# Last projections of a two-layer decoder trunk: a norm's offset kept in PSUM, no GpSimd, and a final product done row by row

## The chip, the cores and the metric

One core of one Trainium2 chip runs the whole kernel in one launch. The time is device microseconds of one execution; for each kernel the median of several runs is given. The profile is of one execution of its own.

## The reference

The input is 1024 tokens of width 1024 in float32. Two layers follow each other; every sub-layer is `x <- LayerNorm(alpha * x + sublayer(x))`, with alpha = 4^0.25. Layer 0 is a sparse attention, layer 1 a gated linear recurrence, and each is followed by a SwiGLU feed-forward of width 2816:

```python
def layer_norm(x, g, b):
    mu = mean(x); var = mean(square(x - mu))
    return (x - mu) * rsqrt(var + 1e-5) * g + b
h = layer_norm(ALPHA * h + mixer(h), ln_g[l, 0], ln_b[l, 0])
h = layer_norm(ALPHA * h + (silu(h @ w_gate) * (h @ w_up)) @ w_down, ln_g[l, 1], ln_b[l, 1])
```

The change concerns the last projection of a sub-layer (`@ w_down`, and `@ w_o` of the recurrence), the residual sum and norm behind it, and the way in which the normalised rows become operands of the next layer's first product.

## The kernel before

All large matrix products after the attention are float32 products made of three matmuls each (`mm3`, lines 103 to 105): both operands are split into a rounded high part (ScalarE, L447) and a rest (VectorE, L448) by `split2`. On top of this, a product is done by a Strassen scheme with 2 x 2 blocks: seven products, numbered 1 to 7, of sums and differences of blocks. `ORDER` and `X` name the operands.

The function `last` does a last projection. It is called three times: for layer 0's feed-forward (11 slices of the inner dimension for each of the seven products), for the recurrence's output projection (4 slices), and for layer 1's feed-forward (11 slices, whose result is the kernel's output). The 1024 tokens are eight rows of 128, `rows[0]` to `rows[7]`; rows 0 to 3 are here called early, rows 4 to 7 late, since the products are taken in the order 1, 2, 6, 5, 3, 7, 4 and the early rows are complete after product 3, the late rows after product 4. Each product runs over slices q, and in a slice over four blocks of rows m, with three matmuls of 128 x 512 each; so a slice is 12 matmuls. For each slice `load` fetches two 128 x 512 blocks, `prepare` splits them two slices ahead, `product` multiplies. The sums go from PSUM into `rows` by VectorE (`scaled`, L714, and `add`, L715); the rows themselves, the residual, are fetched from DRAM (L694), where `keep` (L832) put them.

The norm of the early rows is the generator `leave`, one for each pair of rows. It is advanced by `tick` between slices of products 7 and 4: statistics on VectorE (L790), a reciprocal root of eleven small VectorE steps (`rsqrt`, L113 to L118), one ScalarE pass (L797), then on GpSimd the multiplication by the norm's scale (L800) and the addition of its offset (L801). The row is stored (`keep`, or in the third call into the output, L805), and `features` transposes it on TensorE (L302) and forms Strassen's sums and differences on VectorE (L307), ScalarE and VectorE splitting them for the next product. The late rows go through `norm_late` (L818 to L827), which leaves the offset out of the rows. They are transposed and summed at once by `operand`: transposes of several rows add up in PSUM (L358), and the offset enters by one small product with 12 rows, `off` times `blocks` (L361), built by `parts` (L380 to L395). Because the late rows are kept without offset, the next call of `last` adds it to them on GpSimd (L704), from a broadcast load of it (L700).

In the third call, product 4's last two slices are done row by row: after the matmuls of a row comes its sum, its statistics and its part of `norm_late`.

One queue, SP's, issues all DMAs in order: loads of slices (L655, L656), of rows, of the norm's scale and offset (L709), and the stores. The pool that `last` opens takes memory that the stage before it gives back. The order in which instructions stand on each engine is set by a planner that draws on program order and on its own estimate of durations; it may move work of other parts between the steps of one.

## Time and profile before

| | before |
|---|---|
| median of 3 runs | 2712.49 us (2706.94 to 2715.37) |
| profiled execution | 2713.93 us, its span 2711.7 us |
| TensorE (PE) busy | 2530.6 us, 93% of the span |
| VectorE (DVE) busy | 2002.5 us, 74% |
| ScalarE (ACT) busy | 1130.5 us, 42% |
| GpSimd (POOL) busy | 356.1 us, 13% |
| mean granted TensorE clock | 0.960 |
| first, second, third call of `last`, about | 1115 to 1412, 1866 to 2050, 2441 to 2712 us |

In a line of the profile, the engine is followed by the source line, the operation, the tile that it writes and those that it reads, the shapes and the count. A bracket tells how long the engine was idle before the instruction and what ended that. `x` and `rows` are rows of 128 x 1024; `Y` and `M` are PSUM tiles; `w`, `ph` and `pl` are split operands; `raw` are loaded slices. Names like `DVE rows L715` on the right of an arrow are the instruction whose end was seen last before the waiting engine went on. The matmuls' ends are modelled, so busy shares of PE are read from their starts where it matters.

### The profile page before, as it was taken

Reading aid. Unit: us, or ns where it says so; the run is one execution under the profiler, and the core shown is the slowest. Engines: PE = TensorE matmul, PEld = TensorE weight load, DVE = VectorE, ACT = ScalarE, POOL = GpSimd, SP = SyncE. Lnnn points to the kernel's source line nnn. Section 1 sums busy time; section 2 is a strip of 40 time slices with the busy share of each in tenths; the row PEclk is TensorE's granted clock in tenths of the full one; section 3 lists DMA queues with packets and bytes.
Section 4 is the critical chain, followed back from the end, with each engine's and each line's share of the span. In section 5 each row is a group of like instructions: output and inputs, shape, how many; then the busy total and the mean of one; then the engine's idle time right before and its main releaser. Section 6 shows DMA issues by size and latency. Waiting matters only on the chain.

```text
span 2711.7 us, 36971 instructions
## 1 busy us (share of the span) xinstructions
PE 2530.6 (93%) x13048; PEld 2112.4 (78%) x13048; DVE 2002.5 (74%) x4007; ACT 1130.5 (42%) x2192; POOL 356.1 (13%) x382
## 2 busy tenths in 40 slices
PE   8977899999899999999899999998869999999995
PEld 7765678888888888878788888887658878888774
DVE  6599889643687876656878888887687876664766
ACT  5576667554433233343453333332344323333441
POOL 1333422110000000000302111111130000000011
PEclk9987799999899999999999999999879999999998
DMA  3213210000166753385521111113525763337653
GB/s 130 83 55 126 89 40 25 29 33 10 59 222 240 237 171 117 99 276 197 175 99 71 51 40 67 40 51 109 191 92 181 244 207 116 95 107 252 203 179 132
DMA packets 159665, 334.63 MB, mean 123 GB/s; under 512 B 16593, under 2 KB 47993, under 8 KB 151801
## 3 DMA queue, kind: packets, MB, share of 16 engines
q1 hardware_dynamic: 159480, 332.28, 36.5%
q8 instruction: 103, 1.69, 0.3%
q14 instruction: 82, 0.66, 0.1%
HBM read 233.11 MB, written 99.09 MB: 123 GB/s over the span
## 4 chain that ended last, share of the span: by engine, by line
PE 53%; DVE 16%; DMA 10%; issue 5%; POOL 2%; ACT 2%; SPq 1%; POOLq 0%; DVEq 0%; ACTq 0%
PE M L104 7%; PE M L105 7%; PE M L103 7%; PE Y L104 5%; PE Y L105 5%; PE Y L103 5%; DMA wdt<-in_wd_dram 4%; PE O L1537 4%; DMA t4q<-wdt 3%; DVE w L448 3%; PE Y L961 2%; PE L L1522 2%; DVE wdt L557 2%; PE T L1532 2%; PE Y L358 1%
## 5 line engine op out<-in xcount | busy, mean ns | idle before, releaser
L447 ACT CAST w<-raw 128x512 fp32r<-128x512 f32 (+1 forms) x377 | 292.6, 778 | 501.5 <-PE M L105 250.4
L448 DVE TENSOR_TENSOR w<-raw,w 128x512 fp32r<-128x512 f32 (+1 forms) x377 | 350.5, 932 | 180.5 <-ACT w L447 178.4
L103 PE MATMUL M<-x,w 128*128 128x512 f32 (+1 forms) x1120 | 434.0, 388 | 4.1 <-DVE e L481 2.2
L104 PE MATMUL M<-x,w 128*128 128x512 f32 (+1 forms) x1120 | 430.6, 385 | 0.0
L105 PE MATMUL M<-x,w 128*128 128x512 f32 (+1 forms) x1120 | 427.1, 382 | 2.4 <-DVE w L448 2.4
L103 PE MATMUL Y<-x,w 128*128 128x512 f32 (+1 forms) x644 | 247.5, 385 | 3.9 <-DVE e L481 2.5
L104 PE MATMUL Y<-x,w 128*128 128x512 f32 (+1 forms) x644 | 247.1, 384 | 1.8 <-DVE x L307 1.8
L105 PE MATMUL Y<-x,w 128*128 128x512 f32 (+1 forms) x644 | 246.8, 383 | 0.0
L103 PEld LDWEIGHTS M<-x,w 128*128 128x128 f32 x1120 | 212.0, 189 | 43.9 <-DVE e L481 3.5
L105 PEld LDWEIGHTS M<-x,w 128*128 128x128 f32 x1120 | 212.0, 189 | 41.4 <-DVE w L448 2.8
L104 PEld LDWEIGHTS M<-x,w 128*128 128x128 f32 x1120 | 212.3, 190 | 36.4
L447 ACT CAST w<-s 128x512 fp32r<-128x512 f32 x180 | 111.7, 621 | 307.9 <-PE M L105 87.8
L1537 PEld LDWEIGHTS O<-vv,pT 128*128 128x128 f32 x1152 | 149.2, 200 | 27.3 <-ACT pT L1534 24.1
L1537 PE MATMUL O<-vv,pT 128*128 128x64 f32 x1152 | 155.8, 283 | 5.1 <-ACT pT L1534 4.0
L448 DVE TENSOR_TENSOR w<-s,w 128x512 fp32r<-128x512 f32 x180 | 124.4, 691 | 43.6 <-ACT w L447 43.0
L103 PEld LDWEIGHTS Y<-x,w 128*128 128x128 f32 x644 | 123.0, 191 | 28.4 <-DVE e L481 3.3
L104 PEld LDWEIGHTS Y<-x,w 128*128 128x128 f32 x644 | 123.4, 192 | 25.1 <-DVE x L307 2.0
L105 PEld LDWEIGHTS Y<-x,w 128*128 128x128 f32 x644 | 123.2, 191 | 22.8
L800 POOL TENSOR_TENSOR x<-x,gb 128x1024 f32<-128x1024 f32 x12 | 32.8, 2735 | 792.4 <-ACT x L797 792.4
L1522 PE MATMUL L<-ks,qt 128*128 128x512 f32 (+5 forms) x384 | 116.4, 392 | 19.6 <-DVE nm L1524 18.4
L1534 ACT COPY pT<-T 128x512 f32<-128x512 f32 (+3 forms) x192 | 85.2, 478 | 86.5 <-PE T L1532 85.6
L1526 ACT ACTIVATE p<-p,nm 128x128 f32<-128x128 f32 (+7 forms) x128 | 99.3, 777 | 51.1 <-DVE nm L1524 50.6
(424 smaller groups left out, 5586.3 us busy)
## 6 DMA issues: line engine op xcount, KB each, us to landing
raw<-in_wgu_dram SPq DMA_DIRECT2D x44, 1024.0 KB, 6.8
wdt<-in_wd_dram SPq DMA_DIRECT2D x44, 512.0 KB, 3.9
raw<-in_wd_dram SPq DMA_DIRECT2D x66, 256.0 KB, 3.5
raw<-in_hw_dram SPq DMA_DIRECT2D x16, 1024.0 KB, 4.8
qr<-qd SPq DMA_DIRECT2D x64, 128.0 KB, 2.8
t5q<-wdt SPq DMA_DIRECT2D x26, 256.0 KB, 7.8
t7q<-wdt SPq DMA_DIRECT2D x26, 256.0 KB, 4.6
h7q<-s SPq DMA_DIRECT2D x26, 256.0 KB, 5.8
```

What stands on the lines that cost most here:

```text
L103: mm(out, a[0], b[0], start=first, stop=False, **kw)
L104: mm(out, a[0], b[1], start=False, stop=False, **kw)
L105: mm(out, a[1], b[0], start=False, stop=last, **kw)
L447: self.nc.scalar.copy(hi, x)
L448: (eng or self.nc.vector).tensor_tensor(lo, x, hi.bitcast(F32), op=ALU.subtract)
L557: sub = lambda o, a, b: v.tensor_tensor(o, a, b, op=ALU.subtract)
L961: nc.tensor.matmul(pl[rows, n, cols], lhs, rhs, start=True, stop=True)
L1522: nc.tensor.matmul(ps, s.qt[:, h % 4, :], s.ks[gi][i][:, kr], start=i == 0, stop=i == 1)
L1526: nc.scalar.activation(p, p, AF.Exp, bias=nm, scale=-1.0, accum_out=sm[:, h : h + 1])
L1532: nc.tensor.transpose(pt[:, i * P : (i + 1) * P], p[:, c : c + P], self.ident)
L1534: nc.scalar.copy(pT[:, : m * P], pt[:, : m * P])
L1537: nc.tensor.matmul(po[:, h * 64 : (h + 1) * 64], pT[:, i * P : (i + 1) * P], s.vv[:, k, gi * 64 : (gi + 1) * 64], start=k == 0, stop=k == j,)
```

## The change

In all three calls GpSimd has no more part in it. `features` and `operand` share a helper, `turn`, that transposes terms into one PSUM tile and adds the offset there; so early rows too are kept without it. `leave` is one generator for all four early rows, with one reciprocal root for all; their statistics are taken earlier, as halves of rows become complete (`count`). `norm_row` multiplies by the scale on VectorE (one operation with the mean's subtraction) and by the reciprocal root on ScalarE.

Where the norm before left an offset (the second and the third call), it is no longer added to rows: a second set of `parts`, `plus`, times alpha, enters the PSUM sums of products 2, 5 and 7 by `offset`, four products of 12 rows by 128 columns for each of the four blocks, 48 in a call.

In the second call (`nq < 8`) the early pairs' operands are made by `operand_sum` and `operand_out`, as the late pairs' are, no longer by `features`; the first seven slices are split into the standing weight slots and no longer into the pool's own tiles, and `tick` is called four times a slice instead of three.

In the third call eight of the eleven slices of product 4 are loaded and split during products 2 to 7 (`hold`), into free slots of the operands' memory; then product 4 runs row by row over all eleven slices, each row followed by its own norm, and rows are stored in halves (`norm_out`).

```diff
--- before
+++ after
@@ -286,20 +284,17 @@
-    def features(self, pool, p, rows, defer=False):
-        nc, v = self.nc, self.nc.vector
...
-                y = self.ps_y()
-                ys.append(y)
-                for k in range(4):
-                    o = (4 * i + k) * P
-                    nc.tensor.transpose(y[:, k * P : (k + 1) * P], r[:, o : o + P], self.ident)
+                ys.append(self.ps_y())
+                self.turn(ys[-1], [r[:, i * 512 : (i + 1) * 512]], off[:, i, :])
         while self.owed:
             self.owed.pop(0)()
...
@@ -334,12 +329,25 @@
+    def turn(self, y, terms, off=None):
+        mm = self.nc.tensor.matmul
+        for k in range(4):
+            c = slice(k * P, (k + 1) * P)
+            for i, x in enumerate(terms):
+                flags = dict(is_transpose=True, start=k + i == 0, stop=True, skip_group_check=True)
+                mm(y[:, c], x[:, c], self.ident, **flags)
+        if off is not None:
+            mm(y, off, self.blocks, start=False, stop=True, skip_group_check=True)
     def operand(self, p, n, rows, less, off=None):
-        nc, mm = self.nc, self.nc.tensor.matmul
+        self.operand_out(p, n, self.operand_sum(n, rows, less, off))
+    def operand_sum(self, n, rows, less, off):
         (a1, a2), (b1, b2), (l1, l2) = ((x[:, :512], x[:, 512:]) for x in (*rows, less[1]))
         terms = {
             1: (a1,),
...
@@ -351,14 +359,10 @@
-        for k in range(4):
-            c = slice(k * P, (k + 1) * P)
-            for i, x in enumerate(terms):
...
-            mm(y, off[:, i, :], self.blocks, start=False, stop=True, skip_group_check=True)
+        self.turn(y, terms, None if off is None or n in (4, 5) else off[:, {1: 0, 7: 2}.get(n, 1), :])
+        return y
...
@@ -381,11 +382,20 @@
+    def parts(self, pool, b, tag, scale=None):
...
         nc.sync.dma_start(both[:, 0:2, :], b.rearrange("(i k c) -> k i c", i=2, k=4))
+        if scale is not None:
+            v.tensor_scalar(both[:, 0:2, :], both[:, 0:2, :], scale, None, op0=ALU.mult)
         v.tensor_tensor(both[:, 2, :], both[:, 1, :], both[:, 0, :], op=ALU.subtract)
...
@@ -636,24 +646,31 @@
-        items = [(n, q) for n in (1, 2, 6, 5, 3, 7, 4) for q in range(nq)]
...
+        held = nq - 3 if out else 0
+        items = [(n, q) for n in (1, 2, 6, 5, 3, 7, 4) for q in range(held if n == 4 else 0, nq)]
...
@@ -661,13 +678,28 @@
                 ns = ((2, 3), (), (6, 7), (1, 5))[(len(items) - 1 - i) % 4]
+                if i < 7 and nq < 8:
+                    ns = ((6, 7), (2, 3), (1, 5))[i % 3]
...
+            def hold():
+                for q in range(min(held, 6)):
+                    fetch(spare[q], 4, q)
+                    yield
+                for q in range(held):
+                    x = xs[q // 4][:, q % 4]
+                    self.split2([x[:, 0], x[:, 1]], spare[q % 6])
+                    ready[4, q] = x[:, 0], x[:, 1]
+                    if q + 6 < held:
+                        fetch(spare[q], 4, q + 6)
+                    yield
...
@@ -680,31 +712,41 @@
+                    if n != 1 and q % 3 == 2:
+                        while more and next(more[0], self) is self:
+                            more.pop(0)
...
+            def offset(dst, i):
+                if self.plus is not None:
+                    for k in range(4):
+                        c = slice(k * P, (k + 1) * P)
+                        nc.tensor.matmul(
+                            dst[:, c], self.blocks[:, c], plus[:, i, :], start=False, stop=True, skip_group_check=True
+                        )
...
-            u = self.xslot(0, (P, 4, 512))
+            u = self.xslot(0, (P, 16, 512))
+            spare = [u[:, 4 + 2 * i : 6 + 2 * i] for i in range(6)]
+            if held:
+                xs = [self.xslot(g, (P, 4, 2, 2, 512), F32R) for g in (1, 2)]
+                more.append(hold())
...
+            self.picks(pool)
             if self.plus is not None:
-                w = self.tile(pool, [P, D], F32, "t")
-                nc.sync.dma_start(w, self.plus.partition_broadcast(P))
-                for p in (2, 3):
-                    for i in range(2):
-                        r = rows[p + 4 * i]
-                        gp.tensor_tensor(r, r, w, op=ALU.add)
-            self.plus = gb[1]
+                plus = self.parts(pool, self.plus, "plus", ALPHA)
+            off = self.parts(pool, gb[1], "off") if nxt else None
             wide = []
-            for i, x in enumerate(gb):
+            for i, x in enumerate(gb if out else gb[:1]):
...
@@ -713,7 +755,11 @@
+            stats = self.tile(pool, [P, 8, 2, 6], F32, "lnst")
+            stats = [stats[:, m] for m in range(8)]
+            count = lambda m, i: v.bn_stats(stats[m][:, i, :], rows[m][:, (lo, hi)[i]])
             for m in half:
+                offset(a[m], 0)
                 scaled(rows[m][:, lo], a[m])
...
@@ -727,46 +773,67 @@
+                for m in half:
+                    count(m, 0)
+                    yield
...
-            tick(8)
+            tick(12)
             for m in half:
+                offset(a[m], 1)
                 add(rows[4 + m][:, hi], a[m])
...
             for m in half:
                 add(rows[m][:, hi], a[m])
-            jobs.extend(self.leave(pool, p, [rows[m] for m in self.PAIRS[p]], wide, out) for p in range(2))
+                count(m, 1)
+            jobs.append(self.leave(pool, rows[:4], stats, wide, off, out, nq < 8))
             b = [self.ps_m() for _ in half]
-            pace = (1, 2) if nq > 8 else (3, 3)
+            pace = (1, 2) if nq > 8 else (4, 4)
             products(7, b, ticks=pace)
...
             for m in half:
                 add(rows[4 + m][:, hi], b[m])
-                stats[4 + m] = self.tile(self.small, [P, 2, 6], F32, f"lnst{m}", bufs=1)
-                v.bn_stats(stats[4 + m][:, 1, :], rows[4 + m][:, hi])
+                count(4 + m, 1)
+                offset(b[m], 0)
+            if out:
+                self.plus = None
+                prepare(len(items) - 1)
+                while jobs or more:
+                    tick()
+                    while more and next(more[0], self) is self:
+                        more.pop(0)
+                for m in half:
+                    for q in range(nq):
+                        product(4, q, m, b[m], False)
+                    add(rows[4 + m][:, lo], b[m])
+                    count(4 + m, 0)
+                    p = next(p for p in (2, 3) if 4 + m in self.PAIRS[p])
+                    rs, mv = self.norm_scale([stats[4 + m]])
+                    self.norm_out(rows[4 + m], mv[:, 0, 0:1], rs[:, 0:1], wide, out(4 + m))
+                return
+            self.plus = gb[1]
             few = 2
             products(4, b, True, nq - few, ticks=pace)
...
             for p, rs in zip((2, 3), pairs):
-                self.norm_late(p, rs, [stats[m] for m in self.PAIRS[p]], wide, out)
-                if nxt:
-                    slots = [self.tile(pool, [P, n], F32, x) for n, x in ((512, ("t4", "pl")[p - 2]), (D, ("st", "t")[p - 2]))]
-                    less.append(self.negatives(rs, slots))
+                scale, mv = self.norm_scale([stats[m] for m in self.PAIRS[p]])
+                for i in range(2):
+                    self.norm_row(p + 4 * i, rs[i], mv[:, i, 0:1], scale[:, i : i + 1], wide)
+                less.append(self.negatives(rs, self.less_slots(pool, p)))
...
@@ -774,57 +841,65 @@
+    def less_slots(self, pool, p):
+        return [self.tile(pool, [P, n], F32, x) for n, x in ((512, ("t4", "t5")[p % 2]), (D, ("st", "t")[p % 2]))]
+    def norm_scale(self, stats):
+        n = len(stats)
+        mv = self.tile(self.small, [P, 4, 2], F32, "lnmv")[:, :n]
+        for i, x in enumerate(stats):
+            self.nc.vector.bn_aggr(mv[:, i, :], x.rearrange("p a b -> p (a b)"))
+        return self.rsqrt(mv[:, :, 1], n, 1.0, LN_EPS, "ln"), mv
+    def norm_row(self, i, r, mean, scale, wide):
+        self.nc.vector.scalar_tensor_tensor(r, r, mean, wide[0], op0=ALU.subtract, op1=ALU.mult)
+        self.nc.scalar.activation(r, r, AF.Copy, scale=scale)
+        self.keep(i, r)
+    def norm_out(self, r, mean, scale, wide, dst):
+        v = self.nc.vector
+        v.scalar_tensor_tensor(r, r, mean, wide[0], op0=ALU.subtract, op1=ALU.mult)
+        for c in (slice(0, 512), slice(512, 1024)):
+            v.scalar_tensor_tensor(r[:, c], r[:, c], scale, wide[1][:, c], op0=ALU.mult, op1=ALU.add)
+            self.nc.sync.dma_start(dst[:, c], r[:, c])
+    def leave(self, pool, rows, stats, wide, off, out, summed):
+        scale, mv = self.norm_scale(stats[:4])
...
-        for i, r in enumerate(rows):
-            gp.tensor_tensor(r, r, wide[0], op=ALU.mult)
-            gp.tensor_tensor(r, r, wide[1], op=ALU.add)
-            if out is None:
-                self.keep(p + 4 * i, r)
-            else:
-                nc.sync.dma_start(out(self.PAIRS[p][i]), r)
-            yield
-        if out is None:
-            yield
-            yield
-            yield
-            yield from self.features(pool, p, rows, p == 0)
...
+        pairs = [[rows[m] for m in self.PAIRS[p]] for p in range(2)]
+        less = []
+        for p, rs in enumerate(pairs):
+            for i, m in enumerate(self.PAIRS[p]):
+                if out is not None:
+                    self.norm_out(rs[i], mv[:, m, 0:1], scale[:, m : m + 1], wide, out(m))
+                else:
+                    self.norm_row(p + 4 * i, rs[i], mv[:, m, 0:1], scale[:, m : m + 1], wide)
+                yield
+            if out is None and not summed:
+                yield
+                yield
+                yield from self.features(pool, p, rs, off)
+            elif out is None:
+                less.append(self.negatives(rs, self.less_slots(pool, p)))
+                yield
+                for n in self.ORDER[:-1]:
+                    if p == 0 and n in (1, 5, 7):
+                        self.x_out(0, n)
+                    self.operand(p, n, rs, less[p], off)
+                    yield
+        if less:
+            ys = [self.operand_sum(4, rs, l, off) for rs, l in zip(pairs, less)]
+            self.x_out(0, 4)
+            for p, y in enumerate(ys):
+                self.operand_out(p, 4, y)
...
```

More of the change, by code (lines that the diff above doesn't have):

```diff
@@ L287, in x_in, with features @@
         return x[:, part, i, k, cols]
-    def features(self, pool, p, rows, defer=False):
-        nc, v = self.nc, self.nc.vector
+    def features(self, pool, p, rows, off):
+        nc, v, defer = self.nc, self.nc.vector, p == 0
         ys = []
@@ L353, in operand, with operand_out @@
         y = self.ps_y()
[L354 to L361 removed]
+        self.turn(y, terms, None if off is None or n in (4, 5) else off[:, {1: 0, 7: 2}.get(n, 1), :])
+        return y
+    def operand_out(self, p, n, y):
         x, i = self.X[n]
@@ L370, in negatives, with picks @@
         return slots
-    def parts(self, pool, b):
+    def picks(self, pool):
         nc, v = self.nc, self.nc.vector
@@ L642, in last, with fetch @@
         half = range(4)
-        items = [(n, q) for n in (1, 2, 6, 5, 3, 7, 4) for q in range(nq)]
-        ready, raws, loaded = {}, {}, 0
-        jobs = []
+        held = nq - 3 if out else 0
+        items = [(n, q) for n in (1, 2, 6, 5, 3, 7, 4) for q in range(held if n == 4 else 0, nq)]
+        ready, raws = {}, {}
+        jobs, more = [], []
         with self.tc.tile_pool(name=self.name("la"), bufs=1, reuse_waits="tile") as pool:
-            def load(i):
-                n, q = items[i]
-                if i == 0 or (len(items) - i) % 2 == 0:
-                    self.two = self.tile(self.wp, [P, 2, 2, 512], F32, "raw", bufs=2)
-                raw = raws[i] = self.two[:, (len(items) - i) % 2]
+            def fetch(raw, n, q):
                 w = {1: (0, lo), 2: (1, lo), 3: (1, hi)}.get(n)
@@ L656, in load @@
                 nc.sync.dma_start(raw[:, 1, :], wd[2 * q + w[0]][:, w[1]] if w else wt[q][n])
+            def load(i):
+                if i == 0 or (len(items) - i) % 2 == 0:
+                    self.two = self.tile(self.wp, [P, 2, 2, 512], F32, "raw", bufs=2)
+                raws[i] = self.two[:, (len(items) - i) % 2]
+                fetch(raws[i], *items[i])
             def prepare(i):
@@ L753, in last @@
                 tick()
[L754 removed]
+            first = self.begin(nxt)
             weave(islice(first, 4))
@@ L776, in last @@
             step(half, 9)
-            if nxt:
-                for n in self.ORDER:
-                    for p in (2, 3):
-                        self.operand(p, n, pairs[p - 2], less[p - 2], off)
-    def leave(self, pool, p, rows, wide, out):
-        nc, v, gp = self.nc, self.nc.vector, self.nc.gpsimd
-        n = len(rows)
-        mv = self.tile(self.small, [P, n, 2], F32, "lnmv")
-        for i, r in enumerate(rows):
-            st = self.tile(self.small, [P, 2, 6], F32, "lnst")
-            for c in range(2):
-                v.bn_stats(st[:, c, :], r[:, c * 512 : (c + 1) * 512])
-            v.bn_aggr(mv[:, i, :], st.rearrange("p a b -> p (a b)"))
-            yield
-        rs = self.rsqrt(mv[:, :, 1], n, 1.0, LN_EPS, "ln")
-        mr = self.tile(self.small, [P, n], F32, "lnmr")
-        v.scalar_tensor_tensor(mr, mv[:, :, 0], -1.0, rs, op0=ALU.mult, op1=ALU.mult)
-        for i, r in enumerate(rows):
-            nc.scalar.activation(r, r, AF.Identity, bias=mr[:, i : i + 1], scale=rs[:, i : i + 1])
-        yield
-        for i, r in enumerate(rows):
-            gp.tensor_tensor(r, r, wide[0], op=ALU.mult)
-            gp.tensor_tensor(r, r, wide[1], op=ALU.add)
-            if out is None:
-                self.keep(p + 4 * i, r)
-            else:
-                nc.sync.dma_start(out(self.PAIRS[p][i]), r)
-            yield
-        if out is None:
-            yield
-            yield
-            yield
-            yield from self.features(pool, p, rows, p == 0)
@@ L813, in norm_late @@
-    def norm_late(self, p, rows, stats, wide, out):
-        nc, v = self.nc, self.nc.vector
-        mv = self.tile(self.small, [P, 2, 2], F32, "lnmv")
-        for i in range(2):
-            v.bn_aggr(mv[:, i, :], stats[i].rearrange("p a b -> p (a b)"))
-        rs = self.rsqrt(mv[:, :, 1], 2, 1.0, LN_EPS, "ln")
-        for i, r in enumerate(rows):
-            v.scalar_tensor_tensor(r, r, mv[:, i, 0:1], wide[0], op0=ALU.subtract, op1=ALU.mult)
-            if out is None:
-                nc.scalar.activation(r, r, AF.Copy, scale=rs[:, i : i + 1])
-                self.keep(p + 4 * i, r)
-            else:
-                v.scalar_tensor_tensor(r, r, rs[:, i : i + 1], wide[1], op0=ALU.mult, op1=ALU.add)
-                nc.sync.dma_start(out(self.PAIRS[p][i]), r)
+            for n in self.ORDER:
+                for p in (2, 3):
+                    self.operand(p, n, pairs[p - 2], less[p - 2], off)
```

35 lines of the change are left out of this document (13 added, 22 removed).

## Prediction

> **What bounds the kernel now.** I read four views in this order: the page, the waits of TensorE, the stretches around each wait, and the instructions in order of time there. The page first:
>
> ```profile
> span 2711.7 us, 36971 instructions
>
> L800 POOL TENSOR_TENSOR x<-x,gb 128x1024 f32<-128x1024 f32 x12 | 32.8, 2735 | 792.4 <-ACT x L797 792.4
> ```
>
> TensorE (PE) is busy almost everywhere, and its clock sags in few slices, one group of them late in the middle. So a gain can come only from places where PE stands still or runs at half speed. The waits of PE name them:
>
> ```profile
> PE M L302 <- POOL x L801: 21.8, 4, 12.4
> PE Y L103 <- DVE rows L715: 10.3, 1, 10.3
> PE M L103 <- DVE rows L715: 7.0, 3, 4.7
> PE Y L302 <- POOL x L801: 6.4, 2, 4.6
> ```
>
> All four belong to the three calls of `last`, and the L302 ones wait for GpSimd's (POOL's) scale and offset of early rows. The stretches show what each wait costs (columns: stretch, its length, busy time with instructions of PE, PEld, DVE, ACT, POOL, then granted clock, DMA share, GB/s):
>
> ```profile
> 1319.80:1331.70 11.90, 5.46 (x23) 4.54 (x23) 8.52 (x7) 5.35 (x7) 11.82 (x5) 0.71 0.37 135
> 1398.00:1411.00 13.00, 13.00 (x95) 9.84 (x95) 7.79 (x12) 5.84 (x11) 1.12 (x2) 1.00 0.18 53
> 1914.70:1947.30 32.60, 24.09 (x97) 18.73 (x95) 25.32 (x27) 10.51 (x10) 10.42 (x4) 0.93 0.59 195
> 2639.00:2666.30 27.30, 13.95 (x46) 10.58 (x46) 16.97 (x13) 8.24 (x9) 15.55 (x5) 0.75 0.37 135
> 1961.00:2049.70 88.70, 63.73 (x334) 52.91 (x333) 76.91 (x137) 38.63 (x52) 23.93 (x8) 0.79 0.24 88
> ```
>
> A clock of 0.71 over 11.9 us that is either 1.0 or 0.5 means 2 x 0.29 x 11.9 = 6.9 us at half speed: a wait of PE is paid again behind it. That is my reading of the averages: the clock is halved around the idle time.
>
> **First call** (about 1303 to 1412 us).
>
> ```profile
> 1321.84 1.09 PE L302 MATMUL Y<-ident,x 128*128 128x128 f32 x8 [1.85 <-POOL x L801]
> 1327.53 1.97 PE L302 MATMUL Y<-ident,x 128*128 128x128 f32 x8 [4.59 <-POOL x L801]
> 1404.14 0.66 PE L358 MATMUL Y<-ident,rows 128*128 128x128 f32 x4
> 1404.73 0.38 PE L361 MATMUL Y<-blocks,off 12*128 12x512 bf16 x1
> 1405.04 0.66 PE L358 MATMUL Y<-ident,rows 128*128 128x128 f32 x4
> 1408.36 0.27 PE L358 MATMUL Y<-ident,st 128*128 128x128 f32 x1
> 1408.47 0.27 PE L358 MATMUL Y<-ident,rows 128*128 128x128 f32 x1
> ```
>
> Removed: eight GpSimd operations and with them waits of 1.85 + 4.59 = 6.4 us; of the 6.9 us at half speed some 2.6 are worked in (from 1329.1 on), so 1.3 are lost there. DVE, slowed beside GpSimd, then makes PE wait 2.3 (the 7.0 us listed for L715 less the 4.7 of its longest, which is in the second call). Sum 10.0. Added on PE: the offset goes in by one 512-column product for each of the 8 PSUM tiles of `features`. A transpose takes 0.11 us (1408.36 to 1408.47); four of them and one offset product take 0.90 (1404.14 to 1405.04), so an offset product costs 0.90 - 0.44 = 0.46, eight 3.7 us. DVE takes over one 128x1024 operation a row (4 x 1.25 = 5 us), but loses one of two rsqrt chains and GpSimd's interference, so I leave it at nothing; it is covered by PE's slices: twelve matmuls of 0.227 us, 2.72, of which DVE's own split takes 1.2 (shown below). Net -6.3; bounds -10 (products hidden in remaining waits) and +4 (no wait removed).
>
> **Third call** (from about 2440 us to the end).
>
> ```profile
> 2641.31 0.50 PE L103 MATMUL Y<-ph 128*128 128x512 f32 x1 [2.14 <-ACT ph L447]
> 2662.71 0.76 PE L103 MATMUL Y<-w 128*128 128x512 f32 x1 [10.26 <-DVE rows L715]
> 2651.71 3.20 POOL L801 TENSOR_TENSOR x<-x,gb 128x1024 f32<-128x1024 f32 x1
> 2644.97 10.29 SPq L805 DMA_DIRECT2D out_dram<-x  x3
> 2655.36 0.38 SPq L655 DMA_DIRECT2D raw<-h4q  x1
> 2642.63 10.08 DVE L448 TENSOR_TENSOR w<-raw,w 128x1024 fp32r<-128x1024 f32 x3
> 2666.66 3.54 DVE L448 TENSOR_TENSOR w<-raw,w 128x1024 fp32r<-128x1024 f32 x3
> ```
>
> The wait listed for DVE is really the queue's: on SP the stores of the early rows (L805) wait for GpSimd, and the loads for product 4 stand behind them until 2655.36. DVE meanwhile takes 10.08 us for three splits that take 3.54 once GpSimd is done, 1.2 each. Without GpSimd the stores wait for DVE alone, and eight of the eleven slices are loaded earlier. Gain: 2.14 + 10.26 = 12.4; the clock of 0.75 gives 13.6 us at half speed, of which 6.6 are in the idle time; half of the other 7.0 is lost, 3.5. Sum 15.9. The sixteen DMAs and eight splits of these slices are only moved into the 55 slices of products 2 to 7, each 2.72 us of PE with DVE free for 1.5; if that cover is gone, 8 x 1.23 = 10 us come back.
>
> Added: 48 products of 12 rows by 128 columns, in 12 groups of four. No row has this shape. Nearest is the transpose, also 128 columns, 0.11 us; with a switch to bf16 and back of about 0.15 a group (0.46 less 0.31 until the next start, above) a group is 0.6, a call 7.2 us. Ends: by columns a quarter of the 0.31, 0.08 each, 3.8 us; or the whole 0.46 each, 22 us.
>
> The Trainium skill (TensorE: Matmul & The Clock Gate, Back-to-back issue gap) puts a stream of weight loads with 128-column products at about 81 ns each, whatever the number of rows. An estimate by this page is 3.9 us a call in place of 7.2, and 2671 in place of 2677 for the kernel; no row here shows the shape.
>
> The end itself:
>
> ```profile
> 2694.21 0.40 PE L104 MATMUL Y<-w,w 128*128 128x512 f32 x1
> 2694.44 0.39 PE L105 MATMUL Y<-w,w 128*128 128x512 f32 x1
> 2690.70 0.69 DVE L715 TENSOR_TENSOR rows<-rows,Y 128x512 f32<-128x512 f32 x1 [4.52 <-PE Y L105]
> 1885.05 0.17 DVE L113 TENSOR_SCALAR rmh<-rmq 128x8 f32<-128x8 f32 x1 [1.88 <-ACT vt L1028]
> 1887.07 0.17 DVE L118 SCALAR_TENSOR_TENSOR rmy<-rmt,rmy 128x8 f32<-128x8 f32 x1
> 2705.59 2.48 DVE L826 SCALAR_TENSOR_TENSOR rows<-rows,lny,gb 128x1024 f32<-128x1024 f32 x2
> ```
>
> PE ends at 2694.83; the last DVE operation at 2708.07; the span at 2711.7. So the tail is 16.9 us: 13.2 of norms of four rows and 3.6 for the last store. After the change one row is left when PE ends: add 0.7, statistics 0.7, aggregate 0.2, rsqrt 2.2 (eleven steps, 1885.05 to 1887.24), scale 1.25, two halves 0.7 each: 6.5, and the store's 3.6 (smaller now, so at most that) make 10.1. Each earlier row's 6.5 us hide under the next row's 33 matmuls of 0.23, 7.5 us; were they to take longer, the excess would add up three times. Gain 6.8. Net of the call: -15.9 - 6.8 + 7.2 = -15.5; bounds -24 and +2.
>
> **Second call** (1883 to 2050 us), the hardest.
>
> ```profile
> 1892.58 1.04 ACT L447 CAST ph<-raw 128x1024 fp32r<-128x1024 f32 x1 [7.56 <-DVE vg L1040]
> 1911.04 0.59 SPq L393 DMA_DIRECT2D off<-t  x1
> DVE x L714 <- POOL x L704: 6.7, 2, 4.4
> 2008.17 1.97 PE L302 MATMUL M<-ident,x 128*128 128x128 f32 x8 [12.40 <-POOL x L801]
> L821 DVE SCALAR_TENSOR_TENSOR rows<-rows,lnmv,gb 128x1024 f32<-128x1024 f32 x4 | 9.3, 2324 | 0.0
> L821 DVE SCALAR_TENSOR_TENSOR rows<-rows,lnmv,gb x12: 1231/1283/3381, 1381.0 to 2700.1; 128x1024 f32<-128x1024 f32 x12
> L116 DVE TENSOR_TENSOR lnt<-lny 128x2 f32<-128x2 f32 x12 | 4.9, 410 | 0.0
> ```
>
> Its start: slice 2 waits for the pool that the recurrence held (7.56 us at 1892.58); with the three standing weight slots it can be split before. But the offset's parts are ready only after their last DMA at 1911.04, and now PE needs them behind product 2, which ended at 1914.5 and would end up to 9 us sooner; a second set of parts also stands in SP's queue, ahead of product 6's loads. I take nothing here; ends -9 and +9.
>
> Products 6 and 5 (1914.7 to 1947.3): DVE is the bound, 25.3 us busy and 6.7 idle for GpSimd. Without the 6.7 and with four statistics of 0.7 moved in, 32.6 - 6.7 + 2.7 = 28.6, and PE's own work, eight slices of 2.72 and four offset groups of 0.6, is 24.2. Some of DVE's operations are also freed of GpSimd's interference, so I take -5; ends -7 and 0.
>
> From product 7 on (88.7 us): PE is idle for 88.7 - 63.7 = 25 us; the clock of 0.79 gives 37 us at half speed, 12 outside the idle time, 6 of them lost: 31 to be had. Added to PE: the operands of two early pairs need 112 transposes where 32 were, 80 x 0.11 = 8.8; ten 512-column offsets, 4.6; four groups, 2.4: 15.8. So at best -15. DVE, busy 76.9, loses its slowing (L116's mean of 410 ns against the 0.17 us above, L821's 2324 against the median of 1283: with the other small steps about 15) and some 4 net of its features: 58, below PE's 73. Some waits for norms must remain, so I take half, -8; ends -15 and +5.
>
> In the Trainium skill (TensorE: Matmul & The Clock Gate, Part 4: PE-mode transpose) transposes do not count as activity for the clock, which would speak against this part. The stretch 1398 to 1411 us above, nearly all transposes, kept a clock of 1.00, so the trace does not agree.
>
> **Sum.** -6.3 - 13 - 15.5 = -34.8 on the profiled execution's 2713.9 us (its span and 2.2 us around it), 2679; the median of the runs is 1.4 lower, so 2677. Edits without a price: the broadcast load of the offset gives way in the second and third call to a second set of parts (a load and three small stores on SP and nine short DVE steps; in the third call under product 2, 11 slices of PE; in the second it is the -9 to +9 above); early rows' copies on ScalarE take 1.1 us as before; rsqrt's padded tiles keep their number of steps.
>
> **The rivals.**
> - *More*: the second call's hole before 1893 is filled (-9) and its last stretch comes down to PE's work (-7 more): 2661. For it: PE idle 25 us of 88.7. Against: the queue above.
> - *The second call gives nothing*: PE's 15.8 us and waits for the norm on DVE take the place of GpSimd's: -22, 2690. For it: DVE at 76.9 of 88.7.
> - *The waits only change their name*: the early rows' norm is now on DVE, behind splits, and the transposes and stores wait for it as before; only the tail is saved, less the offset products in the first call: 2709, no change. Against: DVE is free for half of each slice.
> - *Half clock in transposes*: if long runs of transposes do let the clock fall, 224 in the second call take 0.11 us more each, 25 us: 2702. The page above is the rule; the 1.00 speaks against.
> - *Slower*: the small products' price. 96 are added; without them the forecast is -34.8 - 14.4 = -49. Above 49/96 = 0.51 us each the kernel is slower, by 8 us at 0.6: 2720. Against: 0.46 is what four times as many columns cost, at full clock; for it: products of 12 rows between full ones may cost more at half speed.
>
> **Numbers.** Chances: forecast 0.43 (its own range 2666 to 2689), more 0.15, nothing from the second call 0.21, half clock 0.04, names only 0.09, slower 0.08. About 0.3% (8 us) is what a measurement here can tell from no change. Faster: the first four, 0.83; the same 0.09; slower 0.08. The range reaches from a little below the *more* case to the names-only one: 2652 to 2706.
>
> **What would show it.** Right: no wait of PE on GpSimd and a clock near 1.0 in the three calls; no SP stall before product 4's loads; PE's end about 10 us before the span's. Wrong: a wait of PE at the first offset products of the second call; 128-column offset products over 0.2 us apart; a new L715 or `rows` wait of over 5 us at product 4's start; PE waiting between the last rows.

## The result, and the profile after

| | before | after | after, again |
|---|---|---|---|
| median | 2712.73 us (2706.94 to 2715.37) | 2674.72 us (2666.11 to 2682.22) | 2674.44 us, beside 2718.95 before |
| ratio to before, 95% interval | | 0.9848 (0.9823 to 0.9873) | 0.9838 (0.9822 to 0.9855) |
| profiled execution, its span | 2713.93, 2711.7 us | 2682.22, 2680.4 us | span 2669.2 us |
| granted TensorE clock | 0.960 | 0.972 | 0.974 |

The forecast was 2677: 34.8 us less; measured were 38.0 us less (2712.73 - 2674.72). (The ratio in the table is not the quotient of these two medians, which is 0.986.) The page of the changed kernel, and below it its waits of TensorE (engine, line, what it waited for; us in total, times, longest):

```profile
span 2680.4 us, 37329 instructions
PE 2542.1 (95%) x13242; PEld 2115.5 (79%) x13242; DVE 1978.4 (74%) x4025; ACT 1124.5 (42%) x2192; POOL 266.7 (10%) x350
```
```profile
PE M L103 <- DVE e L491: 6.4, 5, 3.5
...
PE M L103 <- DVE rows L757: 4.7, 1, 4.7
...
PE M L103 <- ACT w L457: 3.1, 3, 2.5
PE Y L103 <- ACT ph L457: 2.9, 2, 2.7
PE Y L726 <- DVE rows L757: 2.6, 1, 2.6
```

No wait of the three calls ends on POOL any more; the longest (4.7) is that for the additions ahead of product 3 in the second call. The first wait listed lies in no changed stage: `e` belongs to the first feed-forward layer.

The stretches that answer to the prediction's (columns as there: the end of the first call, where 37 of the 52 matmuls started are transposes; the second call up to its product 3; from its product 7 on; the third call's last rows):

```profile
1407.50:1414.00 6.50, 6.50 (x54) 5.71 (x53) 3.60 (x7) 3.38 (x6) 0.00 (x0) 1.00 0.01 3
1890.60:1936.60 46.00, 40.14 (x180) 31.26 (x178) 34.94 (x49) 14.03 (x14) 0.00 (x0) 0.89 0.74 251
...
1953.10:2031.00 77.90, 71.01 (x444) 55.97 (x444) 60.16 (x122) 38.91 (x57) 0.00 (x0) 0.98 0.27 101
...
2644.00:2670.70 26.70, 26.68 (x119) 21.54 (x118) 17.86 (x52) 0.00 (x0) 0.00 (x0) 1.00 0.14 54
```

From product 7 on the clock is 0.98 where it was 0.79, DVE's 76.9 us have become 60.2 (forecast 58), PE's are 71.0 (forecast 73). Under the last rows PE is never idle.

To compare kernels I cut each profiled execution at instructions that every kernel has: the first copy of `u` in a call (ScalarE, after product 1), the recurrence's first score product and last output, the first SiLU of the second feed-forward layer, PE's last matmul, the span's end. All stage times below are differences of such starts, in us:

| kernel | first call, from `u` | second call, from the recurrence's end | third call, from `u` to PE's end | tail behind PE | all the rest |
|---|---|---|---|---|---|
| before | 249.5 | 158.8 | 201.5 | 16.9 | 2085.0 |
| after | 240.6 | 138.3 | 191.6 | 9.8 | 2100.1 |
| after, again | 239.4 | 136.5 | 191.5 | 9.8 | 2092.0 |
| GpSimd norm undone | 246.5 | 140.7 | 205.1 | 9.4 | 2083.5 |
| `features` again | 240.0 | 136.9 | 190.6 | 9.8 | 2091.9 |
| both of these | 246.4 | 135.9 | 204.4 | 9.4 | 2092.9 |
| four parts undone | 246.4 | 146.2 | 200.0 | 9.5 | 2087.5 |
| five parts undone | 251.6 | 155.0 | 200.6 | 9.4 | 2087.3 |
| pool's tiles again | 241.6 | 138.8 | 190.9 | 9.8 | 2090.2 |
| no offset products | 241.0 | 133.8 | 184.9 | 9.8 | 2095.8 |
| row additions on GpSimd | 241.2 | 136.1 | 186.8 | 9.3 | 2091.4 |
| last product not row by row | 240.5 | 138.3 | 191.6 | 16.8 | 2086.5 |
| late loads | 241.1 | 133.2 | 187.0 | 9.5 | 2093.6 |
| late loads and counts | 240.8 | 132.2 | 187.2 | 9.5 | 2092.5 |

The three calls, with the tail, gained 46 us in the first profile and 50 in the second; the rest lost 15.1 and 7.0.

### The profile page after: what moved, and what is told of

It is laid out like the page before. It is cut to its first block, busy times and chain, and to the rows that moved or that the text cites. A ratio compares the mean times of both kernels' runs of the same rounds, so it can differ in the third digit from the quotient of the medians.

```text
span 2680.4 us, 37329 instructions
## 1 busy us (share of the span) xinstructions
PE 2542.1 (95%) x13242; PEld 2115.5 (79%) x13242; DVE 1978.4 (74%) x4025; ACT 1124.5 (42%) x2192; POOL 266.7 (10%) x350
## 4 chain that ended last, share of the span: by engine, by line
PE 61%; DVE 20%; DMA 11%; issue 4%; ACT 3%; SPq 1%; POOL 1%; DVEq 0%; ACTq 0%; POOLq 0%
PE M L103 8%; PE M L104 8%; PE M L105 7%; PE Y L103 6%; PE Y L105 6%; PE Y L104 5%; PE O L1612 4%; DMA wdt<-in_wd_dram 4%; DMA t4q<-wdt 3%; DVE w L458 3%; PE Y L1036 2%; PE L L1597 2%; PE T L1607 2%; DVE wdt L567 2%; PE Y L339 1%
## 5 line engine op out<-in xcount | busy, mean ns | idle before, releaser
L458 DVE TENSOR_TENSOR w<-raw,w 128x512 fp32r<-128x512 f32 (+1 forms) x373 | 327.8, 882 | 167.0 <-ACT w L457 165.6
L567 DVE TENSOR_TENSOR wdt<-wdt 128x512 f32<-128x512 f32 x104 | 71.8, 691 | 79.1 <-DMA wdt<-in_wd_dram 54.5
```

What stands on the lines that cost most here:

```text
L458: (eng or self.nc.vector).tensor_tensor(lo, x, hi.bitcast(F32), op=ALU.subtract)
L567: sub = lambda o, a, b: v.tensor_tensor(o, a, b, op=ALU.subtract)
```

## The experiments

**The kernel again: is the loss elsewhere part of the change?** No edit.

> The changed kernel again, unaltered, on the same chip as the runs beside it. If the changed stages (the three calls of `last`) gained about 47 us and the 15.5 us that the profiled execution lost in attention, the two feed-forward layers and the recurrence is variation from one execution to the next, then this profile loses another amount in those stages (between 0 and 16 us against the kernel before) while the three calls keep 44 to 50 us, and the time stays near 2675 us. If instead the change itself slows those stages, this profile shows the same 15 us in the same places.

Measured: 2674.44 us, calls 50 us shorter, rest 7.0 longer. The 15 us do not come back. The largest part of them, 8.1 us, lay in the first feed-forward layer (from its first SiLU to the first copy of `u`: 442.0 us before, 450.1 after), and the wait for `e` there is not stable; over the same stretch it is in the kernel before, this run and the run with the pool's tiles again (6.4 us in the first profile of the changed kernel, above):

```profile
PE M L103 <- DVE e L481: 2.2, 3, 1.2
```
```profile
PE M L103 <- DVE e L491: 4.6, 4, 2.3
```
```profile
PE M L103 <- DVE e L491: 1.2, 2, 0.6
```

So it varies between executions: this layer, with the same instructions in the same order on TensorE, VectorE, ScalarE and GpSimd, took 441.1 to 452.4 us in the profiles of the changed kernel and its variants. Whether something systematic of a few us is left stays open: in these thirteen profiles the whole rest lies between 2083 and 2100, mean 2091.2, and there is one profile of before to compare it with, 2085.0.

**GpSimd in the early rows' norm.** In `leave`, for each early row (shortened):

```diff
-self.norm_row / self.norm_out(...)        # VectorE, ScalarE
+nc.scalar.activation(r, r, AF.Identity, bias=mr[:, m : m + 1], scale=scale[:, m : m + 1])
+gp.tensor_tensor(r, r, wide[0], op=ALU.mult)
+if out is not None: gp.tensor_tensor(r, r, wide[1], op=ALU.add)
```

> The changed kernel with the early rows' norm on ACT and GpSimd again (scale and mean on ACT, weight and, in the last call, offset on GpSimd), all else as in the changed kernel. Theory A (GpSimd's place in the chain of the rows made the waits): the second call's product 7 and 4 stretch and the third call's loads behind the stores pay again, 8 to 20 us more, 2683 to 2695. Rival B (with the offset in PSUM and product 4 ordered row by row there is slack, and GpSimd costs nothing on the path): within 3 us of 2675. Rival C (VectorE was the bound in the second call, and freeing it of four rows of 1024 gains): 3 to 6 us less.

Measured: 2692.39 us, ratio 0.9907 (0.9891 to 0.9922), 0.0069 or 19 us above the changed kernel beside it: theory A, of all parts the dearest. By stages +7.1, +4.2 and +13.6 against the kernel again. The third call shows how. SP's queue, then VectorE, then GpSimd, in this kernel's order of time (start, length, instruction):

```profile
2608.58 0.43 SPq L667 DMA_DIRECT2D raw<-t7q  x1
2615.66 17.43 SPq L889 DMA_DIRECT2D out_dram<-x  x4
2633.18 0.38 SPq L666 DMA_DIRECT2D raw<-h7q  x1
```
```profile
2616.64 3.43 DVE L458 TENSOR_TENSOR pl<-raw,ph 128x1024 fp32r<-128x1024 f32 x1
2620.00 3.43 DVE L458 TENSOR_TENSOR w<-raw,w 128x1024 fp32r<-128x1024 f32 x1
2638.31 1.23 DVE L458 TENSOR_TENSOR w<-raw,w 128x1024 fp32r<-128x1024 f32 x1 [14.88 <-ACT w L457]
```
```profile
2610.70 2.43 POOL L886 TENSOR_TENSOR x<-x,gb 128x1024 f32<-128x1024 f32 x1 [639.93 <-DMA raw<-h7q]
...
2615.58 6.76 POOL L886 TENSOR_TENSOR x<-x,gb 128x1024 f32<-128x1024 f32 x2
```

The stores wait 17.4 us for GpSimd, product 7's next load stands behind them until 2633.18, and VectorE has nothing to split for 14.9 us; PE's wait for `w` is 11.5 us. While GpSimd works, a split takes 3.43 us instead of 1.23. In the changed kernel the same point of SP's queue is

```profile
2623.93 0.44 SPq L667 DMA_DIRECT2D raw<-t7q  x1
2625.02 5.53 SPq L871 DMA_DIRECT2D out_dram<-x  x8
2630.60 0.62 SPq L666 DMA_DIRECT2D raw<-h4q  x1
```

Here a load for product 4 stands behind the stores. They still hold the queue, for 5.5 us, and PE does not notice: it is busy without a break from 2588 to 2640 us and, as shown above, under the last rows.

**The transposes' sums in the second call.** `leave(..., nq < 8)` becomes `leave(..., False)`.

> The changed kernel with one part undone: in the second call the early pairs' operands are formed on VectorE and ScalarE from transposed rows (`features`) instead of being summed by transposes in TensorE. Theory A (PE bounds the second call from product 7 on, as the prediction's +15.8 us of added PE work would have it): the second call gets 3 to 9 us shorter. Rival B (VectorE is the bound there): 5 to 12 us longer, with PE waits on VectorE's or ScalarE's x.

Measured: 2672.43 us, ratio 0.9841 (0.9818 to 0.9864); second call 136.9 against 136.5 and 138.3. Neither theory: nothing moves. The stretch from product 3 to the next layer, first in the changed kernel (again), then in this one:

```profile
1932.60:2023.30 90.70, 83.80 (x491) 66.55 (x492) 68.35 (x131) 42.04 (x59) 0.00 (x0) 0.96 0.29 105
```
```profile
1937.20:2027.20 90.00, 78.70 (x408) 61.01 (x409) 71.80 (x135) 40.70 (x56) 0.00 (x0) 0.90 0.31 106
```

83 matmuls and 5.1 us of PE less, 3.5 us of VectorE more, and the difference goes into waits at a lower clock: 90.0 us against 90.7.

**Both undone.** The two edits above together.

> The changed kernel with two parts undone at once: the early rows' norm on GpSimd again and the second call's early operands by `features` again. One by one they moved the second call (from the recurrence's last output to the next layer's first SiLU) from 136 us to 140.1 and 136.3. Theory A (either part removes the wait of the transposes on GpSimd, so undoing one shows nearly nothing and undoing both brings it back): 148 to 156 us in the second call, and 10 to 15 us more than the GpSimd norm alone, a ratio of 0.994 to 0.997. Rival B (the effects add): 140.5 us and 0.991.

Measured: 2690.35 us, 0.9902 (0.9881 to 0.9922); second call 135.9, below the 140.5 of rival B too. (As the table cuts it, the two single figures named in the expectation are 140.7 and 136.9.) My theory A falls: the sums by transposes do not stand in for the missing GpSimd wait. The second call's gain is still not explained.

**Four undone.** With both edits above, the pool's tiles and the row additions on GpSimd (their diffs stand below).

> The changed kernel with the GpSimd norm, `features` in the second call, the pool's tiles for the first splits, and the row additions on GpSimd instead of the offset products, all four undone at once (the early rows' offset is left out, so part of the computation is missing); what stays is the third call's order, the norm's new steps and the moved counts. Theory A (these four are what the second call gained): the second call takes 154 to 160 us, as in the kernel before, whose 158.8 it then accounts for. Rival B (moved counts, the summed generator, or the merged norm of the early pairs hold a part of it): 145 to 152.

Measured: 2695.69 us, 0.9929 (0.9909 to 0.995); second call 146.2, as the rival B said, 12.7 short of the 158.8 of before.

**Five undone: GpSimd's second operation.** In the kernel before GpSimd also added the norm's offset to each early row; the change put that into PSUM. The offset's broadcast load comes back with the addition.

```diff
 gp.tensor_tensor(r, r, wide[0], op=ALU.mult)
+gp.tensor_tensor(r, r, wide[1], op=ALU.add)
-yield from self.features(pool, p, rs, off)
+yield from self.features(pool, p, rs, None)
```

> The kernel with four parts undone, and in it the fifth: GpSimd also adds the norm's offset to the early rows, a second operation of 2.9 us for each row, as in the kernel before (so nothing is left out now), and their operands get none in PSUM. Theory A (the second operation, 4 x 2.9 = 11.5 us of GpSimd in a row, was the larger part of what the transposes waited for): the second call goes from 146 to 154 to 160 us, with PE waits on POOL of 8 us and more between products 7 and 4, and the first call from 246 to 249 or 250; the time is 12 to 18 us more, a ratio of 0.9975 to 1.000. Rival B (what is missing lies in the order of VectorE's work, the counts or the joint generator): the second call 146 to 150.

Measured: 2704.82 us, 0.9957 (0.9939 to 0.9976), 0.0028 or 8 us above four undone; second call 155.0 (+8.8), first call 251.6 (+5.2): theory A by stages, though less than it expected in time. PE's waits on POOL grow; in the second call with four parts undone, then with five, and last in the first call with five:

```profile
PE M L339 <- POOL x L888: 2.6, 2, 1.4
```
```profile
PE M L339 <- POOL x L889: 11.8, 3, 4.8
...
PE Y L339 <- POOL x L889: 5.9, 2, 4.2
```

So the second operation, four times some 2.9 us of GpSimd, is the largest piece that a single edit showed in the second call, with the other four parts undone beside it. 3.9 us (158.8 - 155.0) are left to what stays of the change there (the moved statistics, the joint generator, the pace of `tick`); that was not tried.

The traces settle more when the second call is cut once more, at product 7's first matmul (us up to it, and from it to the next layer's first SiLU):

| kernel | up to product 7 | from product 7 on |
|---|---|---|
| before | 69.2 | 89.6 |
| after | 59.9 | 78.4 |
| after, again | 58.1 | 78.5 |
| GpSimd norm undone | 58.3 | 82.4 |
| both of the first two | 57.6 | 78.2 |
| four parts undone | 65.6 | 80.6 |
| five parts undone | 66.9 | 88.1 |

From product 7 on 11.1 us were gained against the kernel again, and GpSimd's second operation brings back 7.5 of them (80.6 to 88.1). Of the 11.1 gained ahead of product 7, the pool's tiles and the row additions, undone together and without the offset products, bring back 8.0 (57.6 to 65.6).

**The start of the second call: the weight slots.**

```diff
-if i < 7 and nq < 8:
-    ns = ((6, 7), (2, 3), (1, 5))[i % 3]
```

> The changed kernel with one part undone: in the second call the first seven splits go back to the pool's tiles instead of free weight slots. Theory A (the start hole of the second call came from these tiles, and the change closed it by the slots): the copy of product 1 comes 9 to 15 us later than in the changed kernel, and the time rises by 6 to 12 us, to 2681 to 2687. Rival B (the hole closed because POOL no longer adds the rows' offset and the parts come earlier): nothing moves, 2675 within 3 us.

Measured: 2672.64 us, 0.9839 (0.9821 to 0.9858), no difference. As theory A says, the hole does come back, in full: product 1's copy is 9.4 us behind the recurrence's last output, in the changed kernel 5.5 ahead of it. But product 3 starts 47.6 us behind that output against 45.2, and 55.5 before. TensorE's waits from 1880 to 1940 us, with the slots (the kernel again) and without:

```profile
PE M L103 <- DVE rows L757: 5.1, 1, 5.1
PE Y L103 <- ACT ph L457: 2.7, 1, 2.7
PE M L726 <- DMA plus<-t: 0.7, 1, 0.7
```
```profile
PE Y L1111 <- DVE kt L1108: 5.7, 2, 4.3
PE M L103 <- ACT ph L457: 1.9, 1, 1.9
PE M L103 <- DVE rows L755: 1.4, 1, 1.4
```

The waiting moves: PE starts 15 us sooner and then waits for loads and for VectorE's additions. Of the hole's 15 us about 2.4 arrive at product 3, and the times do not show them.

**The row additions on GpSimd.**

```diff
-plus = self.parts(pool, self.plus, "plus", ALPHA)   # and offset(): if False
+nc.gpsimd.tensor_tensor(rows[p + 4 * i], rows[p + 4 * i], w, op=ALU.add)   # four late rows
```

> The changed kernel with the earlier norm's offset added to the four late rows on GpSimd, as the kernel before did, and no offset products at all; the early four rows get no offset, so part of the computation is missing. Theory A (in the kernel before, VectorE stood behind GpSimd's row additions between product 2 and product 3 of the second call): the start of product 3 comes 4 to 8 us later than in the kernel without offset products, with idle of VectorE that ends on POOL; the time is 4 to 10 us above that kernel's ratio of 0.9791, so 0.981 to 0.983. Rival B (the additions have slack): 0.9791 within 0.001.

Measured: 2666.76 us, 0.9813 (0.9789 to 0.9837). Against the kernel without offset products product 3 of the second call starts 4.4 us later (47.7 behind the recurrence's output against 43.3), as A said; at the end of the call 2.3 are left, and the ratios' intervals overlap. In time it is not settled; for the place of the wait, A.

**What the offset products cost.** `offset` does nothing.

> The changed kernel without the small offset products: the earlier norm's offset is left out of the rows in the first to third call where it was added in PSUM, so part of the computation is missing. It prices the products. By the prediction's 0.6 us for each group of four 128-column products over 24 groups: 14.4 us less, 2660. Rival (from the 56 ns between two of these products in the changed kernel's trace): 24 groups of 0.25 to 0.35 are 6 to 8 us, and the two waits at the start of the second call (2.65 and 1.10 us on the parts, with half clock behind them) go as well, 4 to 6: 10 to 14 us less. Without any effect of waits: 6 to 8 less, 2667 to 2669.

Measured: 2660.38 us, 0.9791 (0.9774 to 0.9809), 0.0047 or 13 us less; by stages 9.3 (second call 2.7, third 6.6 with a shorter wait). The waits at the start of the second call, which the rival would have had go, stay; they end on splits now. The trace of the changed kernel prices them directly; a run of sixteen, and four among full matmuls:

```profile
2576.37 0.39 PE L105 MATMUL M<-ph,pl 128*128 128x512 f32 x1
2576.69 1.06 PE L726 MATMUL M<-plus,blocks 12*128 12x128 bf16 x16
2577.96 0.47 PE L103 MATMUL M<-w 128*128 128x512 f32 x1 [0.20 <-ACT ph L457]
2578.26 0.39 PE L104 MATMUL M<-w,w 128*128 128x512 f32 x1
...
2643.75 0.40 PE L105 MATMUL Y<-x 128*128 128x512 f32 x1
2644.08 0.39 PE L726 MATMUL Y<-plus,blocks 12*128 12x128 bf16 x4
2644.41 0.50 PE L103 MATMUL Y<-x 128*128 128x512 f32 x1
2644.74 0.39 PE L104 MATMUL Y<-x 128*128 128x512 f32 x1
```

Start to start the full matmuls are 0.23 apart, but the first one behind a group is followed only after 0.30 to 0.33, so both steps around a group count. Four products add 2644.74 - 2643.75 - 0.46 = 0.53, sixteen 2578.26 - 2576.37 - 0.46 - 0.20 = 1.23: 0.31 to 0.53 for each four, not 0.6. Two products are (1.06 - 0.21)/15 = 0.056 us apart, with the 0.21 us that one is shown to last.

**The last product's order.**

```diff
-held = nq - 3 if out else 0
+held = 0
```

and the final product again slice by slice, its last two slices row by row, the norms behind it.

> The changed kernel with the third call's final product undone: product 4 runs slice by slice over all banks with the last two slices row by row, no slices held in spare buffers, the norm's scale by pairs at the very end, all else as in the changed kernel. Theory A (the tail after the last product is set by that order): the time from PE's end to the span's end goes from 9.75 back to 16.9 us, and the time rises by 7, to a ratio of 0.9865 against the kernel before. Rival B (the norm's two steps and half-row stores alone shorten the tail, the order doesn't matter): tail 9 to 12 us and less than 2 us more. Rival C (held slices also keep PE from waiting for loads): PE's end moves later too, the sum 10 to 18 us.

Measured: 2675.51 us, 0.985 (0.9829 to 0.9871), 0.0012 or 3 us above the changed kernel's 0.9838, a difference that is itself uncertain by 7. The tail goes from 9.8 to 16.8, theory A; PE's end stays (191.6 against 191.5), so the held slices keep PE from no wait. The end of the changed kernel, PE's last matmul and VectorE's first and last operation behind it:

```profile
2670.28 0.40 PE L105 MATMUL Y<-w,w 128*128 128x512 f32 x1
```
```profile
2670.71 0.69 DVE L757 TENSOR_TENSOR rows<-rows,Y 128x512 f32<-128x512 f32 x1 [1.21 <-PE Y L105]
...
2675.60 1.42 DVE L870 SCALAR_TENSOR_TENSOR rows<-rows,lny,gb 128x512 f32<-128x512 f32 x2
```

**Later loads.** Rows 4 to 7, the norm's weight and the parts for the next layer are loaded behind product 2.

```diff
-for r in (self.xslot(3, (P, 4, D)), self.tile(pool, [P, 4, D], F32, "rows")): ...
+bring(self.xslot(3, (P, 4, D)))
 products(2, a, True)
+bring(self.tile(pool, [P, 4, D], F32, "rows"))   # then off, wide
```

> The changed kernel with the loads of rows 4 to 7, of the norm's weight and of the offset's parts for the next layer issued behind product 2 instead of ahead of it. Theory A (after the start hole was filled, PE in the second call waits at 1904 us because 4 MB of row loads at over 300 GB/s and SP's queue hold back the slices of products 1 and 2): the waits of 3.1 and 1.3 us and 3.4 to 6.8 us of half clock go, 4 to 7 us less, ratio 0.981 to 0.9825. Rival B (VectorE's work up to product 3 sets its start, not the loads): the wait goes over to the start of product 3, which begins at the same time, within 1.5 us.

Measured: 2663.54 us, 0.9808 (0.9786 to 0.983): about 8 us (0.0030) below the changed kernel, the intervals overlapping a little. Product 3 of the second call starts 1.5 us sooner (43.7), the edge of rival B: theory A's waits are gone, but smaller ones, 0.8 to 2.3 us and 5.9 in sum, come ahead of product 3. Still the call is 3.3 shorter, and the third call, of which neither theory spoke, 4.5: a wait of 2.5 us for `w` and the 3.4 us of half clock behind it are gone there.

**Later counts too.** The four statistics go behind the additions that product 3 waits for. In the changed kernel they stand ahead of them on VectorE:

```profile
1936.59 2.48 DVE L760 BATCH_NORM_STATS2 lnst<-x 128x6 f32<-128x512 f32 x4
1938.97 2.48 DVE L757 TENSOR_TENSOR rows<-rows,M 128x512 f32<-128x512 f32 x4
```

> The changed kernel with the late loads (ratio 0.9808 by themselves) and with the four statistics of rows 0 to 3 put behind the additions that product 3 waits for. Theory A (VectorE's order sets product 3's start): its wait goes and it starts 1.5 to 3 us earlier after the recurrence's last output than the 43.7 us of the late loads alone; in the third call too; 2 to 4 us less, 0.9795 to 0.980. Rival B (what the counts yielded comes back as waits behind product 3, whose split also needs VectorE): within 1.5 us of 0.9808.

Measured: 2663.96 us, 0.9811 (0.9789 to 0.9833), nothing beside the late loads alone: rival B. Product 3 starts 1.0 us sooner; its wait, 0.9 us with the late loads alone (5.1 in the kernel again), is 0.2, and PE waits up to 2.8 us for a split a little earlier. Both versions are clearly faster than the kernel before; against the changed kernel (0.9838) their gain is at the edge of the noise.

## Why the prediction held, point by point

- **First call**, forecast -6.3 (10.0 removed, 3.7 added): -8.9 and -10.1. The wait was named rightly; putting GpSimd back brings 7.0 (its multiplication) and 5.2 more (its addition), together more than the call had gained.
- **Third call**, forecast -15.5: -16.9 and -17.1. The tail's -6.8 measured -7.1. The small products were mis-sized, 7.2 us a call where the trace has 1.2 + 1.2 + 4 x 0.53 = 4.5. The removed waits and half clock were then a little less than the 15.9: 9.9 (201.5 - 191.6) + 4.5 = 14.4. One step was wrong: the eight slices loaded earlier were a reason in my text for the lost wait, and without them the wait does not return. Taking GpSimd off the stores is enough.
- In the prediction I set the page's 3.9 us beside my 7.2 (the Trainium skill, TensorE: Matmul & The Clock Gate, Back-to-back issue gap). Measured are 4.5 a call, nearer the page's, but by another sum: 0.056 us between two products, which the same section gives as the gap of an isolated one, and 0.15 to 0.17 for each change of shape, where I had put 0.15 for both changes of a group together.
- **Second call, start**, taken as 0 with ends of 9: right in its effect, for a reason I had only half. The hole was filled, 15.6 us of it, and the queue that I named (rows and parts ahead of the slices, at 336 GB/s over 15 us in the kernel again, below) and VectorE took it back before product 3.

```profile
1885.00:1900.00 15.00, 15.00 (x68) 12.09 (x67) 8.78 (x10) 3.29 (x4) 0.00 (x0) 1.00 0.92 336
```

- **Second call, products 6 and 5**, forecast -5: with the hole left as it was, product 3 starts 7.9 us sooner than before (47.6 against 55.5), all of it in products 6 and 5 (24.6 us instead of 32.6), so this term was too small and lies outside its own end of -7. In the two runs without offset products the row additions alone make 4.4.
- **Second call from product 7 on**, forecast -8, half of the 15 to be had: -11.1 (from 89.6 to 78.5, product 7's start to the first SiLU). DVE's relief came as forecast. What failed is the part given to the summed transposes: I charged them 8.8 us of PE against relief of DVE, and undoing them moves the second call by 0.4 us (136.5 to 136.9): no net price and no net gain to be seen. 7.5 of the 11.1 come back with GpSimd's second operation.
- **Rivals.** *More* had its hole filled, and it was worth 2.4 us and not 9. *Half clock in transposes*: clock 0.98 from product 7 on with all 224 transposes in it, and 1.00 in the first call's; it falls. *Waits only change their name* is what became of the filled hole, and of nothing else. *Slower* needed 0.51 us a small product; it is 0.08 to 0.13 with its share of the switch.
- **Signs.** Of those for wrong one came: PE waits at the first offset products of the second call, 1.1 us and, in the kernel again, 0.7, far below the 9 feared. Of those for right one failed in part: the stores still hold SP's queue for 5.5 us ahead of product 4's loads, and the start of the second call is not near full clock (0.89 from 1890.6 to 1936.6 us).
- The forecast was -34.8 and the medians gave -38.0, although the three calls gained 46 to 50 where I had put 34.8, because the stages that I left out of the sum lost 7 to 15 us in the two profiles. The forecast met the time closer than it met the stages, and that was luck; what it had right is the direction of each stage, and GpSimd's place in the early rows as the main cause.

## What to carry to other kernels

An engine that is off the bound still costs when another queue waits for it in order: here stores behind GpSimd held the loads behind them, and in the other two calls TensorE's transposes waited for GpSimd's rows. The two steps that put GpSimd back into the early rows' norm (0.0069 and 0.0028 of the time, 26 us) add up to more than half of what the change gained. Filling a hole at a stage's start pays only as far as the next limit (here row loads and VectorE), so move what stands in that queue first. Undo parts together as well as one by one: in the second call single parts showed 0 to 4 us of a gain of 20 to 22. And cut a stage where the limit changes: the split at product 7 told the two causes apart.

## What was not expected of the hardware

While GpSimd works on 128x1024 rows, a VectorE split of 1.23 us takes 3.43, and GpSimd's own operations go from 2.43 to 3.38 (6.76 for two): each a little under the sum of the two (3.66), as if they took turns. The Trainium skill (SBUF — State Buffer, SBUF: two separate sides) has the rule: a VectorE operation with two inputs in SBUF and a GpSimd operation that reads SBUF contend for a shared port pair, which the one that starts first locks for its whole instruction. These rows agree with it, and beside splits GpSimd's work is not free.

The clock was halved behind short waits too. In the changed kernel's second call PE waits 2.65 us for `ph` and 1.10 us for `plus`, and from the end of the first wait on it runs at half speed for 10.2 us (the last row is the stretch), 9.0 of them busy:

```profile
1910.59 1.22 PE L103 MATMUL Y<-ph 128*128 128x512 f32 x2 [2.65 <-ACT ph L457]
...
1913.84 1.43 PE L726 MATMUL M<-plus,blocks 12*128 12x128 bf16 x12 [1.10 <-DMA plus<-t]
```
```profile
1910.60:1920.80 10.20, 8.96 (x31) 6.50 (x32) 8.02 (x14) 3.14 (x3) 0.00 (x0) 0.50 0.56 160
```

Half of the 9.0, 4.5 us, is lost on top of 3.75 us of waiting, by my estimate from these figures.

The stages outside the three calls took 2100.1 and 2092.0 us in two executions of the same kernel, and 2083.5 to 2100.1 over all its variants; a stage's gain has to be read in the stage, not from the span.
